# Position biases of a neighbourhood attention: 24 short loads and 12 mask adds become 8 run loads and 4 spreading adds, in mid-stage

## The chip, the cores and the metric

The kernel runs on one core of a Trainium2 chip. The metric is the device time of one execution in microseconds (us), taken as the median of several executions.

## The reference

The kernel computes a two-layer encoder over 256 tokens of width 1024, in float32. Each layer is a feed-forward block (width 2816, gated by silu), an attention block and a second feed-forward block, with an RMS norm before and after each and a residual sum. The attention of layer 0 is a differential attention. That of layer 1 is a neighbourhood attention: the tokens form a grid of 4 rows by 64 columns, 16 heads of 64, every query sees all 4 rows and 16 columns near its own, and a relative position bias is added to its scores:

```python
bias = rpb[:, dr[None, :, None], dc[:, None, :]]
sc = jnp.einsum('bqhd,brqjhd->bhqrj', q_row, k_win).astype(jnp.float32) * scale
sc = sc + bias.astype(jnp.float32)[None]
```

`rpb` holds 16 heads x 15 row offsets x 31 column offsets. Only these bias values are concerned here.

## The kernel before

The order of the work is six stages: feed-forward `f10`, attention `a0`, feed-forward `f20`, then for layer 1 `f11`, `a1`, `f21`. Every stage multiplies the activations by weights that stream in from memory. Weights come in pieces of 512 KB. The class `Weights` loads them through SP's DMA queue into tiles `raw` (line 106), which rotate over four buffers (`RAW_BUFS`). ScalarE (ACT) copies each piece, rounded, to `whi` (line 130) and VectorE (DVE) writes the remainder to `wlo` (line 131), each in two instructions of 128x512. These split parts rotate over nine buffers. TensorE (PE) multiplies by both parts. A raw buffer is free again when the second `wlo` has read it, so the next load on SP waits for DVE.

A feed-forward stage begins with four row products (lines 380 to 383) and then goes through column blocks p = 2 to 10 (`gu_cols`, lines 414 and 415: four products into two alternating PSUM banks `mm`; ACT copies half of each bank, line 488, and DVE adds the other half, line 489, which frees the bank). Between the blocks stand the down products (`acc`, line 438).

The biases of eight heads (half of the 16, group g) fit in the tile `bias`, 128 partitions x 8 heads x 6 rows x 64 columns. Partitions 0 to 63 and 64 to 127 are two query rows, with the query columns in reverse order, so that one partition's values are a run of `rpb` that starts one element further than its neighbour's. `queue_bias(g, rate)` makes twelve steps: for each of the six rows j two loads of 64 partitions x 8 heads x 64 elements (line 450) and one add of the mask to `bias[:, :, j]` (line 455). The steps go to a list, `W.extras`. Each time a weight piece is loaded, the next entry of the list is issued after it:

```python
self.n_dma += 1
self.extra(1)
```

`queue_bias(0, 1)` stands ahead of stage `f11` (one step per weight load, so they go out at that stage's start), `queue_bias(1, 3)` inside `a1`, after the last scores of group 0 (three steps per load). What is left of the list is issued at once by `W.extra(len(W.extras))` ahead of the scores that read it (line 641). The order on each engine is otherwise set by the tile framework's scheduler.

Of the kernel before, what the change touches and what calls it, by code (L numbers as in the profile page):

```python
# [9 lines left out]
F32 = mybir.dt.float32  # L10
# [3 lines left out]
ALU = mybir.AluOpType  # L14
# [3 lines left out]
P = 128  # L18
# [11 lines left out]
GRID_W = 64  # L30
LAM_INIT = 0.8 - 0.6 * math.exp(-0.3 * 0)

UE = 1024
# [43 lines left out]
class Weights:  # L77
# [22 lines left out]
    def load(self, upto):  # L100
        nc = self.nc
        while self.n_dma < min(upto, len(self.src)):
            ap = self.src[self.n_dma]
            a, b = ap.shape[1], ap.shape[2]
            t = self.raw_pool.tile([P, UE], F32, tag="raw", name=f"raw{self.n_dma}")
            self.last_dma = nc.sync.dma_start(t[:, : a * b].rearrange("p (a b) -> p a b", b=b), ap)
            self.raw[self.n_dma] = t
            self.n_dma += 1
            self.extra(1)
# [42 lines left out]
def encoder_kernel(ctx, tc, x, norm_g, f1g, f1u, f1d, f2g, f2u, f2d,  # L152
                   dwi, dwo, dlam, dsub, nwi, nwo, rpb, ropec, maskc, out):
    nc = tc.nc
# [4 lines left out]
    raw_pool = ctx.enter_context(tc.tile_pool(name="rawp", bufs=RAW_BUFS))  # L159
# [15 lines left out]
    def nm(s):  # L175
        uid[0] += 1
        return f"{s}_{uid[0]}"

    h = [const.tile([P, D], F32, name=f"h{t}") for t in range(NH)]
    W = Weights(tc, raw_pool, part_pool)  # L180
# [26 lines left out]
    def downs_after(p):  # L207
        if p == 2:
            return [0, 1]
        return [p - 1] if p - 1 < NPAIR - HELD else []  # L210
# [37 lines left out]
    def gain(li, j, queue=nc.sync):  # L248
        t = gp.tile([P, D], F32, tag="gain", name=nm("gain"))
        queue.dma_start(t, bcast(norm_g[li, j, :], P))  # L250
        return t
# [13 lines left out]
    mask = const.tile([P, GRID_W], F32, name="mask")  # L265
# [3 lines left out]
    bias = const.tile([P, 8, 6, GRID_W], F32, name="bias")  # L269
# [172 lines left out]
            for key in keys:  # L442
                W.release(key)

    def queue_bias(g, rate):

        def load(rl, j):
            src = bass.AP(tensor=rpb.tensor, offset=rpb.offset + g * 8 * 465 + (5 - rl + j) * 31 + 16 - GRID_W,
                          ap=[[1, GRID_W], [465, 8], [1, GRID_W]])
            nc.sync.dma_start(bias[rl * GRID_W:(rl + 1) * GRID_W, :, j], src)  # L450

        def add_mask(j):
            l = [list(z) for z in mask.ap]
            mb = bass.AP(tensor=mask.tensor, offset=mask.offset, ap=[l[0], [0, 8], l[1]])
            nc.vector.tensor_tensor(out=bias[:, :, j], in0=bias[:, :, j], in1=mb, op=ALU.add)

        steps = []
        for j in range(6):
            steps += [lambda j=j: load(0, j), lambda j=j: (load(1, j), add_mask(j))]
        W.extras += [steps[i:i + rate] for i in range(0, len(steps), rate)]  # L460

    def ffn(key, li, gpre, xg1, xT, gpost, last):
        accs = [[bank(ps_acc, "acc") for _ in range(2)] for _ in range(NH)]
        hT = {}

        def gu_rows(nme, t):
            ps = mm_tile()
            proj_rows(ps, xT, t, [(key, nme, 0, j) for j in range(KT * NC // UE)])
            return ps

        def act(g):
            s = t2p.tile([P, NC], F32, tag="t2", name=nm("s"))
            nc.scalar.activation(s, g, AF.Silu)
            return s

        def gated(u, s):
            a = t2p.tile([P, NC], F32, tag="t2", name=nm("a"))
            nc.vector.tensor_tensor(out=a, in0=u, in1=s, op=ALU.mult)  # L478
            return a

        def gu_cols(p):
            keys = [[(key, n, p * PW, j) for j in range(KT * PW // UE)] for n in "gu"]
            g = t2p.tile([P, 2, S], F32, tag="t2", name=nm("g"))
            u = t2p.tile([P, 2, S], F32, tag="t2", name=nm("u"))
            for k, y in zip(keys, (g, u)):
                for f in range(2):
                    ps = proj_col(xT, k, f)
                    nc.scalar.activation(y[:, f], ps[:, S:], AF.Copy)  # L488
                    nc.vector.tensor_tensor(out=y[:, f], in0=ps[:, :S], in1=y[:, f], op=ALU.add)  # L489
                if y is g:  # L490
                    s = act(flat(g))
            a = gated(flat(u), s)
            ht = l4p.tile([P, 2, 2, S], F32R, tag="l4", name=nm("hT"))
            split_bank(flat(ht[:, 0]), flat(ht[:, 1]), a)
            for f in range(2):
                hT[2 * p + f] = (ht[:, 0, f, :], ht[:, 1, f, :])

        def down(p, t):
            q = slice(t * P, (t + 1) * P)
            return row_steps(accs[t], lambda i: hT[2 * p + i][0][:, q], lambda i: hT[2 * p + i][1][:, q],  # L500
                             [(key, "d", 2 * p + i) for i in range(2)], p == 0, p == NPAIR - 1, t == NH - 1)

        hh = [l4p.tile([P, 4, S], F32R, tag="l4", name=nm("hT0")) for _ in range(2)]
        for f in range(4):
            hT[f] = (hh[0][:, f, :], hh[1][:, f, :])

        def to_T(a, t):
            q = slice(t * P, (t + 1) * P)
            transpose_split(a, hh[0][:, :, q], hh[1][:, :, q])

        if key == "f10":
            s0 = act(gu_rows("g", 0))
            norm_T(xg1, xT, 1)
            s1 = act(gu_rows("g", 1))
            a0 = gated(gu_rows("u", 0), s0)
        else:
            s0 = act(gu_rows("g", 0))
            a0 = gated(gu_rows("u", 0), s0)
            norm_T(xg1, xT, 1)
            s1 = act(gu_rows("g", 1))  # L520
        to_T(a0, 0)
        a1 = gated(gu_rows("u", 1), s1)
        for p in range(2, NPAIR):
            gu_cols(p)
            if p == 2:
                to_T(a1, 1)
            for d in downs_after(p):
                for t in range(NH):
                    down(d, t)
        for p in range(NPAIR - HELD, NPAIR):  # L530
            down(p, 0)
        xg = norms(0, accs[0], gpost, gpre, True)
        nxT = None if last else xt_tiles("xT")
        for p in range(NPAIR - HELD, NPAIR):
            if p == NPAIR - 1 and not last:
                norm_T(xg, nxT, 0)
            down(p, 1)
        xg = norms(1, accs[1], gpost, gpre, True)
        return xg, nxT

    def attn(key, li, gpre, xg1, xT, gpost):
# [67 lines left out]
        steps = {}  # L609
# [161 lines left out]
        scores(0, 1, 1)  # L771
        probs_T(0, 0, 1)
        if not diff:
            queue_bias(1, 3)
        o = av(0, 0)
        if diff:
            qk_rows(1, 1, 0)
# [43 lines left out]
    xT = xt_tiles("xT")  # L821
# [3 lines left out]
    with tc.issue_after(last_act[0].ins):  # L825
        W.split(4)
        xg1 = first_norm(1, g_first)

    xg1, xT = ffn("f10", 0, gain(0, 2), xg1, xT, gain(0, 1), False)
    xg1, xT = attn("a0", 0, gain(0, 4), xg1, xT, gain(0, 3))  # L830
    xg1, xT = ffn("f20", 0, gain(1, 0), xg1, xT, gain(0, 5), False)
    queue_bias(0, 1)
    xg1, xT = ffn("f11", 1, gain(1, 2), xg1, xT, gain(1, 1), False)
    xg1, xT = attn("a1", 1, gain(1, 4), xg1, xT, gain(1, 3))
    ffn("f21", 1, None, xg1, xT, gain(1, 5), True)

# [41 lines left out]
```

## Time and profile before

| what | value |
|---|---|
| median of 3 runs | 1030.95 us (1029.95 to 1035.32) |
| the profiled execution's own time | 1030.14 us |
| its span, first to last instruction | 1028.4 us |
| PE busy | 98% of the span |
| DVE busy, ACT busy | 65%, 57% |
| mean DMA rate | 179 GB/s |
| bias loads (line 450) | 24, of 128 KB each |
| bias adds (line 455) | 12, of 128x512 |

The span is one execution; what its own time adds to it, 1.7 us, lies outside the first and last instruction. PE is busy almost throughout, so time is lost where PE stands idle or runs slower. Busy shares of the other engines say little by themselves: what counts is whether they release PE in time.

### The profile page before, as it was taken

What the parts mean: (1) busy time and instruction counts of PE and PEld (TensorE: products, weight loads), DVE (VectorE), ACT (ScalarE), POOL (GpSimd) and SP (SyncE); (2) the same over time, 40 slices, a digit from 0 to 9 for tenths busy, and PEclk for the clock granted to TensorE, in tenths of its full rate; (3) what the DMA queues carried; (4) which work ended last, traced back from release to release, by engine and by line L of the source; (5) the groups of instructions that cost most, each with busy time, mean ns of one, the idle gap of its engine ahead of it and who ended that gap; (6) DMA issues with size and microseconds to landing.
All of it is one profiled execution on the core that took longest, in us unless ns stands there. A gap on an engine that the chain in (4) does not pass through costs nothing.

```text
span 1028.4 us, 14692 instructions
## 1 busy us (share of the span) xinstructions
PE 1004.2 (98%) x5342; PEld 844.3 (82%) x5342; DVE 668.0 (65%) x1248; ACT 586.5 (57%) x1235; POOL 22.9 (2%) x38
## 2 busy tenths in 40 slices
PE   8999999999999999999989999999999999999996
PEld 5788888887777788888878888888898878888885
DVE  6766666677767766666666766657865477566662
ACT  6655556567676655556545656545765366555551
POOL 1000000000001000000000000000000010000000
PEclk9999999999999999999999999999999999999999
DMA  8866666374534765666389666646762346665631
GB/s 288 259 197 184 192 187 192 123 237 139 164 104 138 236 200 183 192 188 192 120 209 252 220 183 187 198 128 205 226 174 73 123 144 226 184 199 172 203 103 42
DMA packets 131322, 184.20 MB, mean 179 GB/s; under 512 B 18273, under 2 KB 98145, under 8 KB 131250
## 3 DMA queue, kind: packets, MB, share of 16 engines
q1 hardware_dynamic: 131104, 183.00, 58.3%
q8 instruction: 42, 0.69, 0.3%
q0 software_dynamic: 144, 0.26, 0.2%
q14 instruction: 30, 0.25, 0.1%
q10 hardware_dynamic: 2, 0.00, 0.0%
HBM read 182.19 MB, written 1.05 MB: 178 GB/s over the span
## 4 chain that ended last, share of the span: by engine, by line
PE 85%; DMA 5%; DVE 4%; ACT 3%; issue 1%; POOL 1%; SPq 0%; DVEq 0%; POOLq 0%; ACTq 0%
PE mm L414 25%; PE acc L438 24%; PE mm L415 13%; PE mm L380 5%; PE mm L381 5%; PE mm L383 4%; PE tr L691 2%; PE mm L438 2%; DVE wlo L131 2%; PE tr L365 2%; DMA raw<-in_ffn_wg_dram 2%; ACT whi L130 1%; DMA raw<-in_na_w_in_dram 1%; DMA bias<-in_na_rpb_dram 1%; PE mm L397 1%
## 5 line engine op out<-in xcount | busy, mean ns | idle before, releaser
L131 DVE TENSOR_TENSOR wlo<-raw,whi 128x512 fp32r<-128x512 f32 x656 | 425.2, 687 | 175.9 <-ACT whi L130 166.6
L130 ACT ACTIVATE whi<-raw 128x512 fp32r<-128x512 f32 x656 | 379.6, 624 | 213.7 <-PE mm L414 52.5
L414 PE MATMUL mm<-xT,whi 128*128 128x512 f32 x1152 | 409.7, 400 | 4.7 <-DVE a L478 3.4
L415 PE MATMUL mm<-xT,wlo 128*128 128x256 f32 x1152 | 324.2, 281 | 0.0
L414 PEld LDWEIGHTS mm<-xT,whi 128*128 128x128 f32 x1152 | 217.2, 189 | 59.2 <-DVE a L478 3.8
L415 PEld LDWEIGHTS mm<-xT,wlo 128*128 128x128 f32 x1152 | 218.4, 190 | 1.1
L438 PE MATMUL acc<-whi,hT 128*128 128x512 f32 x704 | 197.2, 391 | 0.0
L438 PEld LDWEIGHTS acc<-whi,hT 128*128 128x128 f32 x704 | 130.2, 188 | 27.1
L380 PE MATMUL mm<-whi,xT 128*128 128x512 f32 x272 | 110.7, 407 | 2.8 <-ACT xT L355 2.7
L438 PE MATMUL acc<-wlo,hT 128*128 128x512 f32 x352 | 111.5, 391 | 0.0
L381 PE MATMUL mm<-wlo,xT 128*128 128x512 f32 x272 | 108.4, 399 | 0.1
L438 PEld LDWEIGHTS acc<-wlo,hT 128*128 128x128 f32 x352 | 66.1, 188 | 14.2
L383 PE MATMUL mm<-whi,xT 128*128 128x512 f32 x272 | 67.4, 390 | 0.0
L380 PEld LDWEIGHTS mm<-whi,xT 128*128 128x128 f32 x272 | 52.1, 191 | 15.8 <-ACT xT L355 5.1
L381 PEld LDWEIGHTS mm<-wlo,xT 128*128 128x128 f32 x272 | 52.0, 191 | 12.0 <-DVE wlo L131 1.7
L383 PEld LDWEIGHTS mm<-whi,xT 128*128 128x128 f32 x272 | 51.1, 188 | 10.6
L489 DVE TENSOR_TENSOR u<-mm,u 128x256 f32<-128x256 f32 x72 | 30.3, 421 | 34.7 <-ACT u L488 34.6
L488 ACT ACTIVATE g<-mm 128x256 f32<-128x256 f32 x72 | 26.9, 374 | 38.4 <-PE mm L415 38.4
L355 ACT ACTIVATE hT<-a 128x512 fp32r<-128x512 f32 x36 | 22.7, 630 | 37.5 <-DVE a L478 37.5
L489 DVE TENSOR_TENSOR g<-mm,g 128x256 f32<-128x256 f32 x72 | 30.3, 421 | 16.1 <-ACT g L488 16.1
L488 ACT ACTIVATE u<-mm 128x256 f32<-128x256 f32 x72 | 27.0, 375 | 19.9 <-PE mm L415 19.9
L356 DVE TENSOR_TENSOR hT<-a,hT 128x512 fp32r<-128x512 f32 x36 | 24.9, 692 | 17.1 <-ACT hT L355 16.1
(113 smaller groups left out, 813.0 us busy)
## 6 DMA issues: line engine op xcount, KB each, us to landing
raw<-in_ffn_wg_dram SPq DMA_DIRECT2D x88, 512.0 KB, 4.6
raw<-in_ffn_wu_dram SPq DMA_DIRECT2D x88, 512.0 KB, 4.5
raw<-in_ffn_wd_dram SPq DMA_DIRECT2D x88, 512.0 KB, 4.3
raw<-in_diff_w_in_dram SPq DMA_DIRECT2D x24, 512.0 KB, 4.5
raw<-in_na_w_in_dram SPq DMA_DIRECT2D x24, 512.0 KB, 4.7
gain<-in_norm_g_dram SPq DMA_DIRECT2D x11, 512.0 KB, 4.8
raw<-in_diff_w_out_dram SPq DMA_DIRECT2D x8, 512.0 KB, 3.5
raw<-in_na_w_out_dram SPq DMA_DIRECT2D x8, 512.0 KB, 3.9
```

What stands on the lines that cost most here:

```text
L130: nc.scalar.activation(hi[:, e], raw[:, e], AF.Copy)
L131: nc.vector.tensor_tensor(out=lo[:, e], in0=raw[:, e], in1=hi.bitcast(F32)[:, e], op=ALU.subtract)
L355: last_act[0] = nc.scalar.activation(hi, ps, AF.Copy)
L356: nc.vector.tensor_tensor(out=lo, in0=ps, in1=hi.bitcast(F32), op=ALU.subtract)
L380: nc.tensor.matmul(ps, xT[0][:, t, kt, :], wh, start=kt == 0, stop=False)
L381: nc.tensor.matmul(ps, xT[0][:, t, kt, :], wl, start=False, stop=False)
L383: nc.tensor.matmul(ps, xT[1][:, t, kt, :], wh, start=False, stop=kt == KT - 1)
L414: nc.tensor.matmul(ps, wh[:, j, c], xT.both(kt), start=kt == 0, stop=False)
L415: nc.tensor.matmul(ps[:, S:], wl[:, j, c], xT.one(0, kt), start=False, stop=kt == KT - 1)
L438: nc.tensor.matmul(ys[b], (xh, xl)[xp](i), parts[i][wp][:, 0, HALVES[b]], start=first and b not in seen, stop=last and left[b] == 0)
L488: nc.scalar.activation(y[:, f], ps[:, S:], AF.Copy)
L489: nc.vector.tensor_tensor(out=y[:, f], in0=ps[:, :S], in1=y[:, f], op=ALU.add)
```

## The change

`queue_bias(g)` now loads, per head and partition, one run of 219 consecutive elements (64 + 5 x 31) in place of six of 64. The runs of four heads go into a tile of the weights' raw rotation (`runs`, two loads of 64 partitions x 4 heads x 219). One add per four heads then reads the six overlapping windows of each run, adds the mask and writes `bias`, 128x1536. Empty entries of the list space these steps out. Per group there are 4 loads and 2 adds instead of 12 and 6. The steps of group 0 are put on the list in stage `f11` after column block p = 5, no longer ahead of the stage; those of group 1 at the same place as before.

```diff
-    def queue_bias(g, rate):
-
-        def load(rl, j):
-            src = bass.AP(tensor=rpb.tensor, offset=rpb.offset + g * 8 * 465 + (5 - rl + j) * 31 + 16 - GRID_W,
-                          ap=[[1, GRID_W], [465, 8], [1, GRID_W]])
-            nc.sync.dma_start(bias[rl * GRID_W:(rl + 1) * GRID_W, :, j], src)
-
-        def add_mask(j):
...
-            nc.vector.tensor_tensor(out=bias[:, :, j], in0=bias[:, :, j], in1=mb, op=ALU.add)
-
-        steps = []
-        for j in range(6):
-            steps += [lambda j=j: load(0, j), lambda j=j: (load(1, j), add_mask(j))]
-        W.extras += [steps[i:i + rate] for i in range(0, len(steps), rate)]
+    def queue_bias(g):
+        run, reach = GRID_W + 5 * 31, 4
+        held = {}
+
+        def load(half):
+            t = raw_pool.tile([P, UE], F32, tag="raw", name=nm("runs"))
+            held[half] = t
+            for rl in range(2):
+                src = bass.AP(tensor=rpb.tensor,
+                              offset=rpb.offset + (g * 8 + half * reach) * 465 + (5 - rl) * 31 + 16 - GRID_W,
+                              ap=[[1, GRID_W], [465, reach], [1, run]])
+                nc.sync.dma_start(t[rl * GRID_W:(rl + 1) * GRID_W, :reach * run].rearrange("p (h r) -> p h r", r=run),
+                                  src)
+
+        def spread(half):
+            t = held.pop(half)
+            rows = bass.AP(tensor=t.tensor, offset=t.offset,
+                           ap=[list(t.ap[0]), [run, reach], [31, 6], [1, GRID_W]])
...
+            nc.vector.tensor_tensor(out=bias[:, half * reach:(half + 1) * reach], in0=rows, in1=m, op=ALU.add)
+
+        W.extras += [[lambda: load(0)], [], [lambda: load(1)], [lambda: spread(0)], [], [lambda: spread(1)]]
...
+            if p == 5 and aside is not None:
+                aside()
...
-            queue_bias(1, 3)
+            queue_bias(1)
...
-    queue_bias(0, 1)
-    xg1, xT = ffn("f11", 1, gain(1, 2), xg1, xT, gain(1, 1), False)
+    xg1, xT = ffn("f11", 1, gain(1, 2), xg1, xT, gain(1, 1), False, lambda: queue_bias(0))
```

How the order moves is shown at three places. In the rows of the change, line 458 is the load of the runs, 467 the spreading add; 487, 498, 652, 684, 686 and 710 are lines 478, 489, 641, 673, 675 and 699 of before.

First, SP's queue at the start of `f11`, before:

```order
L106 DMA raw_5038<-in_ffn_wg_dram 128x4x256
L450 DMA bias<-in_na_rpb_dram 64x8x64
L250 DMA gain_5021<-in_norm_g_dram 128x1024
L106 DMA raw_5047<-in_ffn_wg_dram 128x4x256
L450 DMA bias<-in_na_rpb_dram 64x8x64
L250 DMA gain_5023<-in_norm_g_dram 128x1024
L106 DMA raw_5057<-in_ffn_wu_dram 128x4x256
L450 DMA bias<-in_na_rpb_dram 64x8x64
L106 DMA raw_5066<-in_ffn_wu_dram 128x4x256
L450 DMA bias<-in_na_rpb_dram 64x8x64
L106 DMA raw_5103<-in_ffn_wd_dram 128x1024
```

and in the change:

```order
L106 DMA raw_5038<-in_ffn_wg_dram 128x4x256
L106 DMA raw_5046<-in_ffn_wg_dram 128x4x256
L250 DMA gain_5021<-in_norm_g_dram 128x1024
L106 DMA raw_5054<-in_ffn_wu_dram 128x4x256
L106 DMA raw_5062<-in_ffn_wu_dram 128x4x256
L250 DMA gain_5023<-in_norm_g_dram 128x1024
L106 DMA raw_5097<-in_ffn_wd_dram 128x1024
```

Twelve bias loads no longer stand between the weight loads there, and the two loads of gains come one and two weight pieces later.

Second, DVE at the end of block 5 and the start of block 6 of `f11`, before:

```order
L131 TENSOR_TENSOR wlo_5937<-raw_5841,whi_5936 128x512 x2
L131 TENSOR_TENSOR wlo_5977<-raw_5883,whi_5976 128x512
L489 TENSOR_TENSOR u_5761<-mm_5853,u_5761 128x256
L131 TENSOR_TENSOR wlo_5977<-raw_5883,whi_5976 128x512
L478 TENSOR_TENSOR a_5872<-u_5761,s_5816 128x512
L356 TENSOR_TENSOR hT_5874<-a_5872,hT_5874 128x512
L131 TENSOR_TENSOR wlo_5993<-raw_5891,whi_5992 128x512 x2
L131 TENSOR_TENSOR wlo_6035<-raw_5926,whi_6034 128x512 x2
L489 TENSOR_TENSOR g_5917<-mm_5919,g_5917 128x256
```

and in the change (runs_5913 takes its buffer over from raw_5865):

```order
L131 TENSOR_TENSOR wlo_5925<-raw_5823,whi_5924 128x512 x2
L467 TENSOR_TENSOR bias<-runs_5867,mask 128x1536
L498 TENSOR_TENSOR u_5743<-mm_5835,u_5743 128x256
L131 TENSOR_TENSOR wlo_5966<-raw_5865,whi_5965 128x512
L487 TENSOR_TENSOR a_5854<-u_5743,s_5798 128x512
L131 TENSOR_TENSOR wlo_5966<-raw_5865,whi_5965 128x512
L356 TENSOR_TENSOR hT_5856<-a_5854,hT_5856 128x512
L131 TENSOR_TENSOR wlo_5982<-raw_5876,whi_5981 128x512 x2
L467 TENSOR_TENSOR bias<-runs_5913,mask 128x1536
L131 TENSOR_TENSOR wlo_6025<-raw_5911,whi_6024 128x512
L498 TENSOR_TENSOR g_5902<-mm_5904,g_5902 128x256
```

Two spreads came in, the second ahead of the add that frees a PSUM bank in block 6.

Third, ACT in `a1` about the last copy of the keys (`qk_7455<-mm_7533`; raw_7564 is the fourth piece of the output weights, raw_7731 the fifth), before:

```order
L130 ACTIVATE whi_7749<-raw_7564 128x512 x2
L355 ACTIVATE qk_7455<-mm_7533 128x512
L355 ACTIVATE oT_6809<-tr_7609 128x512
L673 ACTIVATE aT_7621<-tr_7616 128x512
L673 ACTIVATE aT_7635<-tr_7630 128x512
L130 ACTIVATE whi_7878<-raw_7731 128x512 x2
```

and in the change (raw_7547 is the fourth piece, raw_7711 the fifth):

```order
L130 ACTIVATE whi_7729<-raw_7547 128x512 x2
L130 ACTIVATE whi_7858<-raw_7711 128x512
L355 ACTIVATE qk_7445<-mm_7517 128x512
L355 ACTIVATE oT_6799<-tr_7588 128x512
L684 ACTIVATE aT_7600<-tr_7595 128x512
L130 ACTIVATE whi_7858<-raw_7711 128x512
L684 ACTIVATE aT_7614<-tr_7609 128x512
```

Half of the fifth piece's conversion came ahead of the copy of the keys and of the two copies behind it. The load of that piece needs the raw buffer of the second piece, raw_7477, whose second split now stands behind the second spread on DVE:

```order
L710 TENSOR_TENSOR o_7426<-tr_7425,rz_7157 128x256
L131 TENSOR_TENSOR wlo_7706<-raw_7454,whi_7705 128x512
L663 RECIPROCAL rz_7397<-z_7395 128x4
L710 TENSOR_TENSOR o_7426<-tr_7425,rz_7187 128x256
L131 TENSOR_TENSOR wlo_7714<-raw_7477,whi_7713 128x512
L467 TENSOR_TENSOR bias<-runs_7526,mask 128x1536
L356 TENSOR_TENSOR qk_7446<-mm_7447,qk_7445 128x512
L131 TENSOR_TENSOR wlo_7714<-raw_7477,whi_7713 128x512
```

The runs loaded for that spread, runs_7526, in turn take the raw buffer of the first piece, raw_7454.

## Rows read from the trace of the kernel before

**Rows 1.** The page's first part: the span, and one engine's busy time, share, instructions.

```profile
span 1028.4 us, 14692 instructions
PE 1004.2 (98%) x5342; PEld 844.3 (82%) x5342; DVE 668.0 (65%) x1248; ACT 586.5 (57%) x1235; POOL 22.9 (2%) x38
```

**Rows 2.** The chain that ended last, 505 to 552 us: start, us, what.

```profile
523.51 8.71 DMA bias<-in_na_rpb_dram
...
532.92 0.69 DVE wlo L131
...
533.63 3.99 DMA raw<-in_ffn_wd_dram
...
540.26 0.61 DVE a L478
...
540.92 0.50 PE mm L414
```

**Rows 3.** Timelines of DVE and PE there, and a 10 us window (busy, clock, DMA).

```profile
532.31 0.69 DVE L455 TENSOR_TENSOR bias<-bias,mask 128x512 f32<-128x512 f32 x1 [3.54 <-DMA bias<-in_na_rpb_dram]
...
540.92 0.50 PE L414 MATMUL mm<-xT,whi 128*128 128x512 f32 x1 [3.44 <-DVE a L478]
...
540.00:550.00 10.00, 9.08 (x43) 7.94 (x44) 5.87 (x12) 5.01 (x10) 0.00 (x0) 0.83 1.14 245
```

**Rows 4.** Windows, first row product to first down product of f11, f20, f21.

```profile
510.80:551.27 40.47, 36.78 (x177) 30.66 (x176) 26.38 (x45) 19.60 (x41) 1.41 (x2) 0.96 0.92 228
322.21:359.25 37.04, 35.78 (x176) 29.44 (x177) 27.17 (x47) 22.38 (x44) 1.41 (x2) 1.00 0.73 228
833.38:869.66 36.28, 35.74 (x177) 29.27 (x176) 27.65 (x48) 22.20 (x44) 1.41 (x2) 1.00 0.68 217
```

**Rows 5.** Tile bias at 500 to 560 us, then tile bias and tile raw at 740 on.

```profile
DMA to landing us min/median/max: 4.2/7.4/9.5
...
L450 SPq DMA_DIRECT2D bias<-in_na_rpb_dram x12: 595/633/1287, 752.9 to 765.5; - x12
...
DMA to landing us min/median/max: 3.0/3.7/6.4
...
DMA to landing us min/median/max: 3.4/3.7/6.4
```

**Rows 6.** The page's fifth part: two groups of DVE instructions.

```profile
L131 DVE TENSOR_TENSOR wlo<-raw,whi 128x512 fp32r<-128x512 f32 x656 | 425.2, 687 | 175.9 <-ACT whi L130 166.6
...
L489 DVE TENSOR_TENSOR u<-mm,u 128x256 f32<-128x256 f32 x72 | 30.3, 421 | 34.7 <-ACT u L488 34.6
```

**Rows 7.** Timelines of DVE, ACT and PE in blocks 5 and 6 of f11.

```profile
600.88 2.10 DVE L131 TENSOR_TENSOR wlo<-raw,whi 128x512 fp32r<-128x512 f32 x3 [1.18 <-ACT whi L130]
...
606.54 2.10 DVE L131 TENSOR_TENSOR wlo<-raw,whi 128x512 fp32r<-128x512 f32 x3 [1.17 <-ACT whi L130]
...
613.11 2.50 DVE L131 TENSOR_TENSOR wlo<-raw,whi 128x512 fp32r<-128x512 f32 x4 [1.55 <-ACT whi L130]
616.08 0.42 DVE L489 TENSOR_TENSOR g<-mm,g 128x256 f32<-128x256 f32 x1 [0.47 <-ACT g L488]
...
617.01 1.16 ACT L130 ACTIVATE whi<-raw 128x512 fp32r<-128x512 f32 x2 [0.97 <-PE mm L414]
...
618.29 0.40 PE L414 MATMUL mm<-xT,whi 128*128 128x512 f32 x1
```

**Rows 8.** Timelines of DVE, SP's queue, ACT and PE in a1, about the keys of group 1.

```profile
762.74 0.42 DVE L699 TENSOR_TENSOR o<-tr,rz 128x256 f32<-128x256 f32 x1 [0.67 <-PE tr L691]
...
766.21 8.59 SPq L106 DMA_DIRECT2D raw<-in_na_w_out_dram  x4
...
767.39 0.69 DVE L131 TENSOR_TENSOR wlo<-raw,whi 128x512 fp32r<-128x512 f32 x1 [1.72 <-ACT whi L130]
...
774.05 0.60 ACT L355 ACTIVATE qk<-mm 128x512 fp32r<-128x512 f32 x1 [0.41 <-PE mm L399]
...
775.68 0.66 PE L365 MATMUL tr<-ident,p 128*128 128x128 f32 x4 [0.24 <-ACT aT L673]
```

More of the change, by code (lines that the diff above doesn't have):

```diff
@@ L443, in row_steps, with ffn @@
                 W.release(key)
-    def queue_bias(g, rate):
-        def load(rl, j):
-            src = bass.AP(tensor=rpb.tensor, offset=rpb.offset + g * 8 * 465 + (5 - rl + j) * 31 + 16 - GRID_W,
-                          ap=[[1, GRID_W], [465, 8], [1, GRID_W]])
-            nc.sync.dma_start(bias[rl * GRID_W:(rl + 1) * GRID_W, :, j], src)
-        def add_mask(j):
-            l = [list(z) for z in mask.ap]
-            mb = bass.AP(tensor=mask.tensor, offset=mask.offset, ap=[l[0], [0, 8], l[1]])
-            nc.vector.tensor_tensor(out=bias[:, :, j], in0=bias[:, :, j], in1=mb, op=ALU.add)
-        steps = []
-        for j in range(6):
-            steps += [lambda j=j: load(0, j), lambda j=j: (load(1, j), add_mask(j))]
-        W.extras += [steps[i:i + rate] for i in range(0, len(steps), rate)]
-    def ffn(key, li, gpre, xg1, xT, gpost, last):
+    def queue_bias(g):
[14 more added lines that the diff above has]
+                           ap=[list(t.ap[0]), [run, reach], [31, 6], [1, GRID_W]])
+            m = bass.AP(tensor=mask.tensor, offset=mask.offset,
+                        ap=[list(mask.ap[0]), [0, reach], [0, 6], [1, GRID_W]])
+            nc.vector.tensor_tensor(out=bias[:, half * reach:(half + 1) * reach], in0=rows, in1=m, op=ALU.add)
+        W.extras += [[lambda: load(0)], [], [lambda: load(1)], [lambda: spread(0)], [], [lambda: spread(1)]]
+    def ffn(key, li, gpre, xg1, xT, gpost, last, aside=None):
         accs = [[bank(ps_acc, "acc") for _ in range(2)] for _ in range(NH)]
```

## The prediction

> **What bounds the kernel now.** I read the first part of the page first: PE is busy 98% of a span of 1028.4 us [rows 1]. So the change can gain only where PE stands idle or runs below full clock, and lose only where it makes PE wait. Loads or DVE work that come or go elsewhere cost nothing. Second, the chain of waits in `f11`: it runs through a bias load that took 8.71 us, the split of a weight piece behind it, the load of a down piece (3.99 us) and the product of the gate, `a`, to PE [rows 2]. Third, the timelines there: a mask add kept DVE waiting 3.54 us for its load, and PE later stood idle for 3.44 us on `a` [rows 3]. In the 10 us window behind that idle the granted clock is 0.83: at the half level (1.2 GHz for 2.4) that is 10 x 0.17 = 1.7 us lost [rows 3]. Fourth, the same stretch of the three feed-forwards of one shape: 40.47 us in `f11`, which has the bias steps, and 37.04 and 36.28 us in `f20` and `f21`, which have none and clock 1.00 [rows 4]. That is the prize. Last, the two places into which the steps move: blocks 5 and 6 of `f11` [rows 7], and `a1` about the keys of group 1 [rows 8]. I ask of each what now stands ahead of work that PE needs.
>
> **The start of f11.** Twelve loads leave SP's queue and six adds leave DVE's. What is left has the order of `f20` and `f21`, so the stretch should fall from 40.47 to between 37.04 and 36.28: a gain of 3.4 to 4.2 us, and I take 3.8. This already holds the idle 3.44 us and the half-clock stretch behind it; neither is counted again. The other way, the raw buffers could still be late: as a rival below.
>
> **What a spread costs.** No row of before has one. An instruction of 128x512 takes 687 ns, one of 128x256 takes 421 [rows 6], which is 266/256 = 1.04 ns for each further element; 128x1536 is then 0.687 + 1024 x 1.04 ns = 1.75 us. The other bound is three separate instructions, 2.06 us. I take 1.75, since it is one instruction. On DVE, four spreads (7.0 us) replace twelve adds (8.2 us); as DVE is 65% busy, the total decides nothing, the place does.
>
> **What a run load costs.** The two loads of a pair go out 0.63 us apart (the issue time of the bias loads) and land some 3.7 us later: the median of bias loads in `a1`, and of raw loads too, with ends of 3.0 and 6.4 [rows 5]. The bias loads' 7.4 at the start of `f11` was twelve of them among a new stage's first weights [rows 5]; mid-stage has no such queue, so I take 3.7.
>
> **Blocks 5 and 6 of f11.** The first pair, `runs_5867`, takes the buffer whose second split ends at 600.88 + 1.3 = 602.2 [rows 7]. It lands by 602.9 + 3.7 = 606.6. DVE reaches the spread two splits into the burst that began at 606.54, at 607.9: no wait. The spread ends at 609.6. The work behind it then follows closely: the add of `u` (610.0), a split of `raw_5865` (610.6), the gate product (611.2), the second split (611.9). PE is in its down products in that time and nothing there is late, by the order.
>
> The second pair waits on SP for that last split, since `runs_5913` takes over the buffer of `raw_5865`. It goes out at 611.9 and 612.5 and lands at 616.2. DVE is done with the splits ahead of it two splits after 613.11, at 614.4 [rows 7], and so waits 1.8 us. The spread ends at 617.95, the split behind it at 618.55, and the add that frees a PSUM bank at 618.95. Before, that add ran at 616.08, and PE takes the next bank at 618.29 [rows 7]. PE so waits **0.7 us**. The bounds: nothing, if the pair lands in 3.0; 1.3, if the second of a pair is later by another issue time of 0.63. Behind the waiting load on SP stand weights: the next one goes out at 613.1 and lands at 616.8, for a conversion that ACT began at 617.01 [rows 7]: covered. The one that takes the buffer of `runs_5913` goes out at 618, after the spread, and has a block's time before it is needed.
>
> **a1, the first spread of group 1.** It stands where a split of 0.69 us stood, ahead of a copy that PE's second block of attention products reads. It delays that by 1.75 - 0.69 = 1.06 us; DVE then waited 0.67 us for PE anyway [rows 8]. So it costs between nothing and 0.4 us; I take nothing, since what PE reads next is a block of products away.
>
> **a1, the second.** `runs_7526` takes the buffer of `raw_7454`, whose split follows the add of 762.74 [rows 8]: it ends at 763.16 + 0.61 = 763.8. The pair goes out at 763.8 and 764.4 and lands at 768.1. Before, DVE was at the same split as early as 767.39 [rows 8]. The spread ends at 769.85, the key copy behind it at 770.45, and the second split of `raw_7477` at 771.1. Only then can the fifth piece of the output weights go out on SP, where before the last four went out from 766.21 [rows 8]. It lands at 774.8, and in ACT's new order half of its conversion (0.6 us) stands ahead of the copy of the keys, which so begins at 775.4, not at 774.05 [rows 8]: 1.35 us late. PE waited on ACT there already, by 0.24 us until 775.68 [rows 8], so no cover is left but some 0.4 us of score products that PE's order now has ahead of the waiting transposes. I take **1.0 us**, with bounds of nothing (the scheduler's order covers it) and 3.7 (the piece lands in 6.4, as the slowest raw load there did). The four adds that leave DVE in this stretch save PE at most that 0.24.
>
> **The sum.** -3.8 + 0.7 + 1.0 = -2.1 us against the profiled execution's own 1030.14 gives 1028.0; the median of the runs shown stands 0.8 above that execution. The bounds together: -4.2 gives 1025.9, and -3.4 + 1.3 + 3.7 = +1.6 gives 1031.7.
>
> **A rule of the Trainium skill.** The trace has 3.7 us at the median and 3.0 at the least for loads of 128 KB, issue to landing [rows 5]. The page "DMA: Bandwidth & Descriptors" ("Anatomy of one DMA — SWDGE (gpsimd) path") gives one transfer 2.0 us and its bytes over 436 GB/s, a fit for another issuing path than SP's: an estimate of 2.5 us for the 224 KB of a run load (64 x 4 x 219 x 4 bytes), and of 3.2 for a piece of 512 KB. By that the runs would land at 615.0, no bank would be late, the fifth piece would come 0.5 earlier, and the sum would be -3.3, 1026.8. The rows are above the page in both sizes (3.4 is the least for raw), so the sum goes by the rows.
>
> **The rivals.**
>
> *Faster, both new waits hidden.* The run loads land at the short end, 3.0, and the piece in 3.4 [rows 5]. Then the spread in `f11` starts at 615.5 and the bank is free at 618.3, on time; in `a1` 0.7 us stays. The sum is -3.8 + 0.7 = -3.1, **1027.0**; with the larger prize and no stall in `a1` it goes to 1025.9. For it: raw and bias loads compete less with twelve short loads gone. Against it: a run load is 1.75 times a bias load's bytes. Chance 0.25.
>
> *The change doesn't free the start.* The raw buffers at the start of `f11` are held by splits that wait on ACT and on PE, not on DVE's adds alone; DMA is busy 0.92 of that stretch [rows 4], and a late down piece could leave half of the idle time. Then the sum is -1.9 + 0.7 + 1.0 = -0.2, **1029.9**. Against it: the chain names the bias load, and two stages of the same shape run without the idle. Chance 0.15.
>
> *Slower: the fifth piece in a1.* If it lands in 6.4 us after its late issue, ACT's queue holds keys, transposed outputs and probabilities behind its conversion, and PE stands idle for 1.0 + 2.7 = 3.7 us. An idle of 3.44 us was followed by a stretch at half clock that cost 1.7 [rows 3], so this one may cost 5.4. The sum is -3.8 + 0.7 + 5.4 = +2.3, **1032.4**. It decides from a wait of 3.1 us on, a landing 5.8 us after the issue. For it: the 6.4 was measured in this very stretch [rows 5]. Against it: the twelve loads that filled the queue then are four now. Chance 0.10.
>
> **How the numbers follow.** The forecast, 1028.0, has the remaining 0.50. The range takes in it, the faster rival and the unfreed start, with the bounds above: 1025.5 (0.4 under the lowest sum, for the 0.24 us of PE idle in `a1` and the spread of runs) to 1031.7. What is left out is the slower rival and ends that fall together. Half a per cent, 5.15 us, is about what a measurement of this kernel can tell from no change; every sum above lies within it of 1030.95 but the lowest (1025.9) and below. So faster has 0.10, the same 0.85, and slower, which needs the slower rival with a second loss in `f11`, 0.05.
>
> **What the profile of the changed kernel would show.** Right: the stretch to the first down product of `f11` at 36.3 to 37.0 us, no idle over 1 us on PE in it and clock 1.00 behind it; spreads of some 1.75 us; run loads landing after some 3.7; the second spread of `f11` waiting about 1.8 us for its load, and PE idle about 0.7 us at the first products of block 6's second bank; in `a1`, ACT's copy of the keys held up by the conversion of the fifth output piece, and PE idle by about 1.0 us more than 0.24. Wrong: a stretch still near 39 us with PE waiting on `a`; run loads landing well under 3 or over 5 us; spreads over 2.1 us; a half-clock stretch in `a1`; or a new wait of over 1 us anywhere else in `f11` after block 5.

## The result, and the profile after

The change runs in 1023.73 us (median of 8) against 1030.45 us before in the same session: a ratio of 0.9938, interval 0.9919 to 0.9957. Two of the eight runs of before, 1998 and 3398 us long, were disturbed; without them its median is 1029.5, and the change stands 5.8 us below that. A second session gave 0.9956 (0.9938 to 0.9974). Over both intervals that is 3 to 8 us faster; the forecast was 2.1 us. The profiled execution's span is 1022.0 us, where [rows 1] has 1028.4. The page's first part after:

```profile
PE 1002.6 (98%) x5342; PEld 842.8 (82%) x5342; DVE 667.3 (65%) x1240; ACT 586.3 (57%) x1235; POOL 22.9 (2%) x38
```

DVE's total is what it was, and so is the mean DMA rate (179 GB/s). Where did the time go? Three stretches of the trace answer it, each as a row of the view of windows (the stretch, its length, busy time and count of PE, PE's weight loads, DVE, ACT and POOL, the granted clock, DMA share, GB/s). First the whole of `f11` and of `a1` before, from one stage's first row product to the next stage's:

```profile
510.80:702.81 192.01, 188.32 (x961) 159.55 (x960) 126.10 (x217) 105.88 (x210) 2.51 (x4) 0.99 0.68 195
702.81:833.38 130.57, 127.69 (x858) 111.16 (x856) 83.64 (x200) 75.89 (x183) 2.83 (x4) 1.00 0.50 155
```

Then after: the start of `f11` (it answers to the first of [rows 4]), `f11`, `a1`, and the 10 us that were at clock 0.83 in [rows 3]:

```profile
511.56:547.26 35.70, 35.35 (x177) 29.39 (x176) 27.58 (x47) 22.86 (x48) 1.42 (x2) 1.00 0.77 255
511.56:698.80 187.24, 186.89 (x962) 158.38 (x960) 125.94 (x213) 105.99 (x211) 2.52 (x4) 1.00 0.65 196
698.80:828.67 129.87, 127.16 (x857) 111.22 (x856) 83.23 (x196) 75.86 (x183) 2.83 (x4) 1.00 0.48 150
...
540.00:550.00 10.00, 9.90 (x55) 8.31 (x54) 8.79 (x17) 7.62 (x16) 0.00 (x0) 1.00 0.91 291
```

`f11` is 4.77 us shorter, and all of it lies before the first down product: 40.47 to 35.70. From there to the end of the stage both kernels take the same time to a hundredth (151.54 us). The idle of 3.44 us and the half-clock stretch behind it are gone: in the stretch PE's idle time falls from 3.69 us (40.47 - 36.78) to 0.35, and its busy time, for the same products, by 1.43 us (36.78 to 35.35). `a1` is 0.70 us shorter, which the experiments put down to scatter. Another 1.7 us of the 6.4 between the two spans lie in `f21`, which the change doesn't touch: 195.0 us before, 193.3 after, and 193.2 to 194.0 in every other profiled execution here.

The places into which the steps moved, in the change's timelines (start, us, engine, line, what, and in brackets the idle time before it and what ended it). DVE in blocks 5 and 6 of `f11`, PE's first product into the freed bank, and SP's queue (they answer to [rows 7]):

```profile
604.20 1.76 DVE L467 TENSOR_TENSOR bias<-runs,mask 128x1536 f32<-128x1536 f32 x1 [0.38 <-DMA runs<-in_na_rpb_dram]
...
610.89 1.76 DVE L467 TENSOR_TENSOR bias<-runs,mask 128x1536 f32<-128x1536 f32 x1 [0.50 <-DMA runs<-in_na_rpb_dram]
...
613.16 0.42 DVE L498 TENSOR_TENSOR g<-mm,g 128x256 f32<-128x256 f32 x1
...
614.27 0.40 PE L414 MATMUL mm<-xT,whi 128*128 128x512 f32 x1
...
605.98 1.27 SPq L458 DMA_DIRECT2D runs<-in_na_rpb_dram  x2
```

The second pair goes out at 605.98, as the first spread ends (604.20 + 1.76), and not after the splits that follow it. So DVE waits 0.50 us for it, not 1.8, and the add that frees the bank ends at 613.58, 0.7 us before PE takes it at 614.27. PE waits for nothing.

In `a1`, DVE, SP's queue, ACT and PE (they answer to [rows 8]):

```profile
754.77 1.75 DVE L467 TENSOR_TENSOR bias<-runs,mask 128x1536 f32<-128x1536 f32 x1
...
763.31 1.75 DVE L467 TENSOR_TENSOR bias<-runs,mask 128x1536 f32<-128x1536 f32 x1
...
756.55 1.27 SPq L458 DMA_DIRECT2D runs<-in_na_rpb_dram  x2
...
765.09 0.33 SPq L106 DMA_DIRECT2D raw<-in_na_w_out_dram  x1
...
769.24 0.64 ACT L130 ACTIVATE whi<-raw 128x512 fp32r<-128x512 f32 x1 [0.29 <-PE mm L398]
...
771.38 0.80 PE L365 MATMUL tr<-ident,p 128*128 128x128 f32 x5 [0.29 <-ACT aT L684]
```

Again the second pair goes out as the first spread ends (756.52). The fifth output piece goes out when the second spread ends (765.06), lands in time, and its conversion on ACT waits 0.29 us for PE, not for the piece. PE's own wait behind it is 0.29 us, and was 0.24 [rows 8].

### The profile page after: what moved, and what is told of

Read it like the earlier page. It is cut to its first block, busy times and chain, and to the rows that moved or that the text cites. A ratio compares the mean times of both kernels' runs of the same rounds, so it can differ in the third digit from the quotient of the medians.

```text
span 1022.0 us, 14666 instructions
## 1 busy us (share of the span) xinstructions
PE 1002.6 (98%) x5342; PEld 842.8 (82%) x5342; DVE 667.3 (65%) x1240; ACT 586.3 (57%) x1235; POOL 22.9 (2%) x38
## 4 chain that ended last, share of the span: by engine, by line
PE 87%; DMA 4%; ACT 4%; DVE 3%; issue 1%; POOL 0%; SPq 0%; DVEq 0%; POOLq 0%; ACTq 0%
PE mm L414 25%; PE acc L438 24%; PE mm L415 13%; PE mm L380 5%; PE mm L381 5%; PE mm L383 5%; PE mm L438 2%; PE tr L365 2%; PE tr L702 2%; DMA raw<-in_ffn_wg_dram 2%; DVE wlo L131 2%; DMA raw<-in_ffn_wu_dram 1%; ACT whi L130 1%; DMA raw<-in_na_w_in_dram 1%; PE mm L397 1%
```

## The experiments

All stage times are those of the profiled execution, from first row product to first row product ("start of f11": to its first down product). Ratios are against runs of the kernel before on the same chip. A star marks an `a1` with a granted clock under 1 in a 10 us window between 730 and 750 us.

| kernel | start of f11 | f11 | a1 | ratio of times |
|---|---|---|---|---|
| before | 40.47 | 192.01 | 130.57 | 1 |
| the change | 35.70 | 187.24 | 129.87 | 0.9938 (0.9919 to 0.9957) |
| the change again | 35.67 | 187.22 | 130.08 | 0.9956 (0.9938 to 0.9974) |
| group 0 new, mid-stage | 35.70 | 187.24 | 130.21 | 0.9959 (0.9944 to 0.9975) |
| group 0 old, mid-stage | 35.74 | 187.30 | 131.91* | 0.9941 (0.9921 to 0.9961) |
| group 0 new, at the start | 41.36 | 192.91 | 131.96* | 0.9993 (0.9976 to 1.0009) |
| group 1 new alone | 40.83 | 192.37 | 132.00* | 0.9986 (0.9968 to 1.0003) |
| group 0 old, adds late | 39.06 | 190.61 | 129.66 | 0.9973 (0.9959 to 0.9988) |
| group 0 loads on POOL's queue, adds late | 41.60 | 193.14 | 129.42 | 0.9993 (0.9975 to 1.0011) |
| group 0 adds only | 37.66 | 190.45 | 132.12* | 0.9947 (0.9928 to 0.9967) |
| group 0 adds only, again | 37.43 | 189.31 | 129.49 | 0.9959 (0.9908 to 1.0009) |
| second spread twice | 36.05 | 187.59 | 130.71 | 0.9957 (0.9936 to 0.9978) |
| second pair later | 35.82 | 187.37 | 129.59 | 0.9953 (0.9936 to 0.9969) |
| no biases | 35.93 | 187.48 | 129.78 | 0.9929 (0.9904 to 0.9954) |

**Form against place.** The change does two things to group 0: another form of loads and adds, and another place. Four kernels separate them. In each, `queue_old` is the function of before. In the first three group 1 is as before; the first has group 0 as in the change:

```diff
-            queue_bias(1)
+            queue_old(1, 3)
```

> Group 0 as in the change (runs, mid-stage), group 1 as before. If the whole gain sits at the start of f11: the stretch from the first row product to the first down product of f11 takes 35.7 to 36.3 us instead of 40.47, blocks 5 and 6 keep their 16.79 us a block, a1 keeps its 130.6 us, and the time is 4.5 to 5 us below before. Rival, that a1 carries a share of its own: the time is only 3.5 to 4.5 us below before, and the kernel with group 1 alone shows the rest.

The second has group 0's old form in the new place (and the edit above):

```diff
-    xg1, xT = ffn("f11", 1, gain(1, 2), xg1, xT, gain(1, 1), False, lambda: queue_bias(0))
+    xg1, xT = ffn("f11", 1, gain(1, 2), xg1, xT, gain(1, 1), False, lambda: queue_old(0, 1))
```

> Group 0 in the old form (twelve loads, six adds) but put on the list after column block 5, group 1 as before. Place theory: the loads hurt only at the stage's start, so the start stretch falls to 35.7 to 36.3 us and the middle costs 0 to 1 us; time 4 to 5 us below before. Form theory: twelve short loads and six waiting adds cost as much wherever they stand, so 3 to 5 us of PE idle come back in blocks 5 to 8; time within 1.5 us of before.

The third has the new form in the old place (and the first edit):

```diff
-    xg1, xT = ffn("f11", 1, gain(1, 2), xg1, xT, gain(1, 1), False, lambda: queue_bias(0))
+    queue_bias(0)
+    xg1, xT = ffn("f11", 1, gain(1, 2), xg1, xT, gain(1, 1), False)
```

> Group 0 in the new form (four loads, two spreads) but at the start of f11 as before, group 1 as before. Place theory: the runs take raw buffers from the first weights and the spreads wait on DVE for their loads there, so 2 us or more of the 4.8 remain and the start stretch stays over 37.5 us. Form theory: four loads instead of twelve do it, and the stretch falls to 35.7 to 36.5 us.

The fourth has group 0 as before, and group 1 as in the change:

```diff
-    xg1, xT = ffn("f11", 1, gain(1, 2), xg1, xT, gain(1, 1), False, lambda: queue_bias(0))
+    queue_old(0, 1)
+    xg1, xT = ffn("f11", 1, gain(1, 2), xg1, xT, gain(1, 1), False)
```

> Group 1 alone in the new form, group 0 as before. The forecast had a1 1.0 us longer (131.6 us from its first row product to that of f21, before 130.57). The profile of the change had 129.87; if that is the change's doing, 129.9 here, if it is the scatter of one execution to the next, 130.2 to 130.9. The start stretch of f11 stays at 40 us or more in every case; time within 1 us of before.

For the length of `f11` the place decides, with either form. The old form in mid-stage has the change's `f11` within 0.06 us. The new form at the stage's start has no gain at all, and its start stretch is even 0.9 us longer than before. What PE waited for there, in the kernel with the new form at the start:

```profile
543.59 0.80 PE L414 MATMUL mm<-xT,whi 128*128 128x512 f32 x1 [3.90 <-DVE a L504]
```

It is the same wait as in [rows 3], on the gate product, now 3.90 us. The second spread waits on DVE for its runs there, with splits behind it, longer than the add of [rows 3] did:

```profile
533.09 1.76 DVE L484 TENSOR_TENSOR bias<-runs,mask 128x1536 f32<-128x1536 f32 x1 [4.88 <-DMA runs<-in_na_rpb_dram]
```

The runs also stand in the weights' raw buffers: the stage's next `wg` piece goes out 7.0 us after the first row product (519.54), where before it was 4.5 (515.33). How much of the loss is the 4.88 us and how much the buffers has not been separated.

The middle costs the old form nothing either: each of its blocks takes 16.79 us (one add there waits 1.5 us for its load, and nothing behind it is late for PE). And `f11` with group 0 new is 187.24 us whether group 1 is new or old, so the steps of the two groups do not meet. By its runs the first kernel is 4.2 us below before (0.9959), which its rival, a share for `a1`, had also allowed; the kernel with group 1 alone can't tell such a share from none.

Group 1 alone gave 132.00 us in `a1`, over every length that had been expected. But kernels with the old group 1 have this length too, see below; its time, 0.9986, can't be told from no change.

**Loads or adds.** The chain of [rows 2] names a bias load, an add behind it and the splits behind the add. Which of the two does the harm: the add that waits on DVE, or the loads? In the next kernel, the twelve old loads stay at the start, and the adds are tied behind an add of block 5:

```diff
+            W.extras += [[lambda rl=rl, j=j: load(rl, j)] for j in range(6) for rl in range(2)]
+            def behind(j):
+                with tc.issue_after(W.dve.ins):
+                    add_mask(j)
+            return [[lambda j=j: behind(j)] for j in range(6)]
...
+    late = queue_old(0, 1)
+    xg1, xT = ffn("f11", 1, gain(1, 2), xg1, xT, gain(1, 1), False, lambda: W.extras.extend(late))
```

> Group 0's twelve old loads stay at the start of f11, but their six adds stand on DVE in blocks 5 and 6; group 1 as before. If what cost the start is the add that waits on DVE ahead of the splits: the start stretch falls to 35.7 to 36.5 us, PE's idle of 3.4 us on the gate product is gone, time 4 to 6 us below before. If it is the loads themselves, in SP's queue and on the DMA engines: the stretch stays over 38.5 us and the time within 2 us of before.

The stretch came out at 39.06 us, as the second expectation has it: with no add there, 3.4 of the 4.8 us stay. The time, 0.9973, is 2.8 us below before, more than the 2 us that were allowed. No add waits there any more, and the chain shows a down piece that takes 7.44 us to land (it took 3.99 in [rows 2], but was issued 3.9 us later then, behind the waiting add: 533.63 against 529.69):

```profile
529.69 7.44 DMA raw<-in_ffn_wd_dram
```

Either way the piece landed at 537.1 to 537.6, and PE waited on `a`. Counted from the stage's first row product it landed 26.8 us in before and 26.0 here. And in the chain of before one more add stands directly ahead of the gate product:

```profile
539.66 0.60 DVE bias L455
```

The 0.8 and 0.6 us are the 1.4 us by which the stretch fell (40.47 to 39.06). Is the rest the loads' place in SP's queue, 0.6 us of issue each, or their traffic? The same kernel with group 0's loads on POOL's queue:

```diff
-            nc.sync.dma_start(bias[rl * GRID_W:(rl + 1) * GRID_W, :, j], src)
+            if g == 1:
+                nc.sync.dma_start(bias[rl * GRID_W:(rl + 1) * GRID_W, :, j], src)
+            else:
+                with tc.issue_after(W.pool.ins):
+                    nc.gpsimd.dma_start(bias[rl * GRID_W:(rl + 1) * GRID_W, :, j], src)
```

> Group 0's twelve old loads at the start of f11 on POOL's own DMA queue, behind the stage's last norm, and not on SP's between the weights; adds in blocks 5 and 6; group 1 as before. If a load hurts by standing in SP's queue ahead of weight loads (0.6 us of issue each): the start stretch falls from the 39.06 us of the kernel with the adds late to 35.7 to 36.5. If it hurts by its small pieces on the 16 DMA engines, whichever queue they come from: it stays at 38 us or more, with the down piece's load again at 7 us or so.

The start took 41.60 us. SP issued its weights undisturbed (0.33 to 0.38 us each; before, some took up to 1.88), and still the down piece took 9.33 us to land:

```profile
530.68 9.33 DMA raw<-in_ffn_wd_dram
```

The down piece that the change issues at this point, 530.18, landed in 3.4 us, with no bias load under way:

```profile
DMA to landing us min/median/max: 3.4/3.4/3.4
```

So a place in SP's queue is not needed for the harm; what the two kernels share is twelve short loads under way beside the weights. POOL sends them in one burst from 521.0 to 532.3, closer together than SP did (510.9 to 546.0 in the kernel with the adds late). That may be why this kernel loses 2.5 us more; whether POOL's queue has a price of its own has not been run.

Last, the adds without the loads (group 0's loads are left out, the adds work on zeros):

```diff
+            if g == 1:
+                nc.sync.dma_start(bias[rl * GRID_W:(rl + 1) * GRID_W, :, j], src)
...
+            with tc.issue_after(W.lo.ins):
+                nc.vector.tensor_tensor(out=bias[:, :, j], in0=bias[:, :, j], in1=mb, op=ALU.add)
```

> Group 0's six adds stand at the start of f11 as before, but its twelve loads are left out (the adds work on a bias tile set to zero once, so they never wait); group 1 as before. If the loads are the cause and DVE's own time for the adds is free: the start stretch is 35.7 to 36.5 us. With the loads kept and the adds moved it was 39.06, with both 40.47. Rival, that six times 0.6 us of DVE work ahead of the splits cost by themselves: 37 us or more.

> The kernel with group 0's adds at the start of f11 and no loads of that group once more: its one profiled execution had f11 3.2 us longer than the change (190.45 against 187.24 us), while its timed runs stand 5.5 us below before, as low as the change's. If the adds' own DVE time costs 3 us, f11 is near 190.4 us again; if that execution was an odd one and the loads carry nearly all of the price, 187.3 to 188.5.

Two profiled executions gave `f11` 3.2 and 2.1 us over the change's. In both, PE waits 1.7 us for a split, once, early in the stage, and there are smaller waits later. In the first of them (its lines are one further down than before's):

```profile
515.36 0.68 DVE L458 TENSOR_TENSOR bias<-bias,mask 128x512 f32<-128x512 f32 x1
...
519.70 0.68 DVE L131 TENSOR_TENSOR wlo<-raw,whi 128x512 fp32r<-128x512 f32 x1
...
520.43 0.51 PE L382 MATMUL mm<-wlo,xT 128*128 128x512 f32 x1 [1.73 <-DVE wlo L131]
```

The split that PE waits for is the fourth behind the add. In before the four stand ahead of the scaling `xg` of the stage's norm (from 519.88); here the add at the head moves the fourth behind `xg`, and PE waits. So the rival of the first expectation held for the stretch: 37.66 and 37.43 us, where it had 37 or more. Of the second neither side did: `f11` is 189.31 us, between 188.5 and 190.4. But without loads to wait for, the scheduler puts the first adds earlier than they stood before (there the first ran at 522.41, behind these splits). And the times don't settle the size: the median of the first set, 1026.73, is 3.0 us below before's 1029.7 of that session, its ratio of 0.9947 makes it 5.5, and the second set's interval (0.9908 to 1.0009) takes in both. This much is shown: an add of 0.6 us that waits for nothing can hold PE up there, by the order in which the splits come behind it. The parts (3.4 us with the loads alone, 1.7 to 2.0 with the adds alone, in this order) add up to more than the 4.77 us of the stretch, so they are not independent prices.

**The prices of the waits in mid-stage.** Two kernels put a load on the terms of the forecast. The second spread twice:

```diff
-        W.extras += [[lambda: load(0)], [], [lambda: load(1)], [lambda: spread(0)], [], [lambda: spread(1)]]
+        W.extras += [[lambda: load(0)], [], [lambda: load(1)], [lambda: spread(0)], [], [lambda: (spread(1, True), spread(1))]]
```

(`True` keeps the runs for the second copy.)

> The change, with the second spread of each group executed twice in a row (the same values written again), 1.67 us more on DVE at both places. From the profile of the change: in f11 the add behind it ended at 613.58 and PE took the bank at about 614.27, a slack of 0.7 us; so PE idles 1.0 us there and that block takes 17.8 us instead of 16.79. In a1 the fifth output piece goes out 1.67 us later (766.8), lands about 770.4, and ACT's copy of the keys is 1.2 us late: PE idles 0.7 to 1.2 us more. Rival, that there is more cover at both places than the rows show: both stay as they are, and the time is that of the change.

The second pair later:

```diff
-        W.extras += [[lambda: load(0)], [], [lambda: load(1)], [lambda: spread(0)], [], [lambda: spread(1)]]
+        W.extras += [[lambda: load(0)], [], [], [lambda: load(1), lambda: spread(0)], [], [lambda: spread(1)]]
```

> The change with the second pair of run loads one weight piece later on the list, which gives it the raw buffers that the forecast had assumed in the change (that of the wg piece of block 6 in f11, that of the first output piece in a1). The forecast's prices: block 6 of f11 0.7 us longer (17.5 instead of 16.79) and a1 1.0 us longer (about 131 without a dip of the clock). From the trace of the change: the slack ahead of the bank is 0.7 us and the fifth output piece has 0.5 us of ACT's wait on PE as cover, and the scheduler puts the spread behind the add that frees the bank; so both stay: 16.79, and a1 129.8 to 130.3.

Neither cost anything in the middle of `f11`: every block stays at 16.79 us. The first did not test what it was meant to: the scheduler put the second copy behind the add that frees the bank, and not in a row with the first, so no bank was late (its 36.05 us at the start is a wait of 0.30 us in a place that the edit doesn't touch). In `a1` too it stood apart; 130.71 us is 0.14 over before's own 130.57, and PE has no wait there that the change lacks. The second is the forecast's own situation with the buffers: there the pair goes out only at 610.58, as the split it waits for ends, and DVE waits 1.20 us for it:

```profile
614.99 0.42 DVE L498 TENSOR_TENSOR g<-mm,g 128x256 f32<-128x256 f32 x1 [0.47 <-ACT g L497]
616.62 1.76 DVE L467 TENSOR_TENSOR bias<-runs,mask 128x1536 f32<-128x1536 f32 x1 [1.20 <-DMA runs<-in_na_rpb_dram]
```

The add of the bank now stands ahead of the spread, and PE loses nothing; `a1` is 129.59 us. So the forecast's 0.7 and 1.0 us are not paid even with its buffers, since the order changes with them. What a late spread ahead of the bank's add would cost has not been run.

**The floor.** All bias work left out:

```diff
+    nc.gpsimd.memset(bias, 0.0)
-            queue_bias(1)
+            pass
-    xg1, xT = ffn("f11", 1, gain(1, 2), xg1, xT, gain(1, 1), False, lambda: queue_bias(0))
+    xg1, xT = ffn("f11", 1, gain(1, 2), xg1, xT, gain(1, 1), False)
```

> All bias loads and mask adds are left out (the scores of a1 read a bias tile set to zero once at the start). If the change has already taken the whole price of the biases off PE's path: f11 187.2 us and a1 129.9 to 132 us as in the runs so far, time within 1 us of the change. Rival, that the run loads and spreads still cost something in blocks 5 and 6 or in a1: 1 to 3 us below the change, seen in that stage.

> The change once more, beside the others. The start stretch of f11 35.7 us, the blocks 16.79 us, by every theory. For a1, two lengths have been seen, 129.9 to 130.6 and 131.9 to 132.0 us, with either form of group 1: if the form of group 1 decides, 129.9; if it is the wait at the stage's first scores (0.4 to 0.5 us in the short ones of the later kernels, 0.7 to 1.0 in the long ones) and the clock behind it, either, with a granted clock under 1 in the long one.

`f11` 187.48 and `a1` 129.78 us: the change is at this floor in both (187.24 and 187.22, 129.87 and 130.08). So in the profiled executions nothing of the biases is left on PE's path in these stages. The times are less sharp: the four runs without biases (median 1023.03) stand 0.7 us below the change's first session, as expected, but 2.7 us below the ten runs of the change beside them (1025.68). The intervals overlap, and no stage shows the difference as a wait on a bias step, so it is left open whether any of it is the biases'.

**Group 1 and the length of a1.** With the old group 1 and clock 1.00, `a1` took 130.57, 130.21, 129.66 and 129.42 us, and 129.49 with the adds alone. With the new one it took 129.87, 130.08, 129.59 and, the second spread doubled, 130.71; without biases 129.78. So no cost of the old form's twelve loads and six adds shows there beyond the scatter, and the new form had nothing to gain. The starred ones, 131.9 to 132.1, are of both forms. They have a window at a lower clock, as here in the kernel with group 1 new alone:

```profile
740.00:750.00 10.00, 8.51 (x65) 7.81 (x64) 6.15 (x25) 7.13 (x20) 0.00 (x0) 0.83 0.60 203
```

## Why the prediction was wrong

The direction and the place of the gain were right; the size was not. Against the profiled execution, the steps that the change touches moved by -4.77 us in `f11` and by nothing that can be told from scatter in `a1`; 1030.14 - 4.8 is 1025.4. The forecast had -2.1: it took 1.0 us too little at the start of `f11` and charged 1.7 us for two waits that did not come. What the first session has beyond 4.8 us is not the change's doing as far as the rows show: 1.7 us between the two profiled executions are `f21`'s, and the second session has -4.5 us (0.9956).

- **The start of f11, -3.8: right in kind, too small.** It measured -4.77. The step that failed is "the stretch should fall from 40.47 to between 37.04 and 36.28". The stretches of `f20` and `f21` are not a floor: they hold waits of their own, 37.04 - 35.78 = 1.26 and 36.28 - 35.74 = 0.54 us more than PE's busy time [rows 4]; the change's `f11` has 0.35. Its own rows would have been nearer: the idle of 3.44 and the 1.7 us at half clock [rows 3] make 5.1. Those two were in the text, which said that its 3.8 already held them; 5.1 does not fit into 3.8. As measured, PE's idle in the stretch fell by 3.34 us and its busy time by 1.43.
- **A spread, 1.75 us: right** (1.756 us at the median; the forecast had it from the slope of two shapes). **A pair lands in some 3.7 us: right** (3.5 to 5.1, median 3.8). The Trainium skill's page "DMA: Bandwidth & Descriptors" ("Anatomy of one DMA — SWDGE (gpsimd) path") would have had 2.5 us, as an estimate from a fit for another issuing path; no load of runs came under 3.5.
- **Blocks 5 and 6, +0.7: not paid.** The step that failed is "the second pair waits on SP for that last split, since `runs_5913` takes over the buffer of `raw_5865`". It took over the buffer of the first pair, and went out as the first spread ended. The same note in the part on the change was mistaken, and so was the one on `runs_7526`. The trace shows it in two ways: the pair goes out at 605.98, when the first spread has ended (604.20 + 1.76), and its issue waits for the semaphores of both loads of the first pair, where the issue of a weight piece behind another waits for the one load that filled its buffer. I had counted buffers in the order of the program, and the built order gave them out otherwise. With its own buffer the order would have moved as well: in the kernel with the second pair later the add of the bank went ahead of the spread.
- **a1, +1.0: not paid.** The same step failed, on "`runs_7526` takes the buffer of `raw_7454`": the pair went out at 756.55, 2.6 us ahead of the end of the split that I had it wait for (759.19). The fifth piece did go out 2.9 us later than before, counted from the stage's start (765.09 - 698.80 against 766.21 - 702.81), and had cover: ACT's conversion waited for PE, not for it. It went out as the second spread ended (765.06) and not behind the second split of `raw_7477`: it took the buffer of that pair of runs. That PE waited on ACT there already was right (0.29 for 0.24 us), and so was the first spread's cost of nothing.
- **The rivals.** "Both new waits hidden" is what happened, but not for its reason: the loads did not land at 3.0. "The change doesn't free the start" did not come, since with no bias load beside it the down piece landed in 3.4 us; the slower one did not, since the fifth piece had cover. Three side sums were off. A pair that lands earlier in `a1` also lets the second spread begin 0.7 us earlier (767.39 for 768.1), so by the forecast's own rows the faster rival comes to -3.8 and not -3.1. A run load has 1.71 times a bias load's bytes, not 1.75. And 1025.9 still lies within 5.15 us of 1030.95. None of them moves the forecast. By the same step as the faster rival, the sum given under "A rule of the Trainium skill" comes to -3.8 and not -3.3.
- **The cause of the old loss** was told as a chain from one bias load over one add. The runs say that the loads under way are enough for 3.4 of the 4.8 us without any add, and from either queue (39.06 and 41.60 us), and that the place among the first weights of the stage is what both forms share when they lose.

## What to carry to other kernels

Here extra loads and adds cost where the weights themselves come late, at the start of a stage, and nothing that shows in its middle: first look where a stage has slack, and only then at how many instructions the extra work takes. To price what goes away, take the idle and the clock loss of that very stretch; a sibling stage has waits of its own. Before a wait is put into a sum, read from the built order which earlier load and which reader it waits for, and what the order moves ahead of it: counting a pool's buffers by hand gave both wrong terms here.

## What was not expected of the hardware

- With twelve loads of 128 KB in pieces of 256 bytes under way, one and the same weight load of 512 KB took 7.44 and 9.33 us to land, with SP's queue free in the second case; without them, in the change, it took 3.4. In mid-stage twelve such loads, 4.3 to 7.1 us to landing, held PE up nowhere.
- Every profiled execution in which PE stood idle for 2.08 us or longer on `a` in `f11` (before and four of the kernels) has a 10 us window at clock 0.83 or 0.66 behind it (3.4 or 6.8 us at the half level of 1.2 GHz), and none of the others has. In `f10` PE has a wait on `a` too: of 2.19 to 3.39 us in eight executions, all with such a window behind it, and of 1.30 to 2.02 in the other six, none with one. In `a1`, whose first score products wait for ACT and DVE one after the other, the clock fell in the executions where the first of these waits was 0.75 to 1.03 us, and not where it was 0.73 or less. There it cost some 2 us (131.9 to 132.1 against 129.4 to 130.7), whichever form group 1 had, so it is part of the scatter between single executions. These are lengths that were seen; no kernel was run to find a bound.
